# Strassen parts inside w1 at another byte distance from their stationary operand, and w2's own Strassen chunks one chunk later

## The chip, the cores and the metric

One Trainium2 chip, one core. The metric is device time in microseconds of one execution of the program.

## What is computed

Two transformer layers on 256 tokens of width 2048, all in float32: layer 0 mixes with stick-breaking attention, layer 1 with a sparse attention of three branches. Each layer ends with the same kind of MLP, which is where the change lies:

```python
def sqrelu_mlp(h, w1, w2):                      # w1: 2048 x 8192, w2: 8192 x 2048
    return jnp.square(jax.nn.relu(h @ w1)) @ w2

for layer in range(2):
    h = h + mixer(rms_norm(h, norm_g), ...)
    h = h + sqrelu_mlp(rms_norm(h, mlp_norm_g[layer]), mlp_w1[layer], mlp_w2[layer])
```

## The kernel before

Weights stream from HBM in chunks of 512 KB: a chunk is a tile `raw` of 128 partitions x 1024 floats (two blocks of 128 rows by 512 columns). ScalarE writes a rounded copy `hi`, VectorE the rest `lo = raw - hi` (`split`), and TensorE takes the product from three matmuls in fp32r: hi by the activations' high part, hi by their low part, lo by their high part. The pools hold five `raw`, four `hi` and four `lo` tiles.

Each MLP runs four feed-forward groups `fg` of 2048 columns. `group1(fg)` multiplies by w1: four blocks of eight chunks in `chunk_T`, each 24 matmuls at L186 with the weights as the **stationary** operand (128x128) and the activations `xs` as the **moving** one (256 columns). `group2(fg)` multiplies by w2 in `chunk_N`, 12 matmuls at L156 with the activations `yhi`, `ylo` stationary and 512 columns of the weights moving. Two of w2's four column blocks of each group are computed with a Strassen scheme instead: `chunk_S`, 21 matmuls at L253 with activations stationary (`yhi`, `ylo`, or prepared sums `ss`) and 256 columns of weights or of weight sums moving. Below, a *w1 chunk* is one call of `chunk_T`, an *N chunk* one of `chunk_N`, an *S chunk* one of `chunk_S`.

S chunks are never run in a row. Block 3 of group `fg - 1` is run inside `group1(fg)`, for fg of 1 to 3: `proj_T` calls `step` after the third and the sixth chunk of each block, so eight S chunks lie between 32 w1 chunks. Block 2 is run inside `group2(fg)`, between N chunks, at positions that the line with `j >= ...` sets (L464). An S chunk costs VectorE five operations (L226, L232, L233, L234 `slo`, and L136 on `ts`), ScalarE two (L231 `shi`, L134 on `ts`); `shi` and `slo` have one buffer each.

Every `hi`, `lo`, `shi` and `slo` tile has 64 spare elements (`PAD`), and its data begin at an offset into the tile:

```python
PAD = 64
NEAR, FAR, TURN, SUM, SUM0 = 0, 16, 8, 48, 60       # elements of 4 bytes
```

These tiles are a whole number of 256 bytes long in each partition, and so are all rows and columns that a matmul steps over, so the offset sets where stationary and moving operand lie towards each other, modulo 256 bytes. In the built program, as stationary start minus moving start modulo 256 bytes (the *distance* below): N chunks 0 (NEAR), w1 chunks 64 (FAR), the first w1 chunk of a `group1` with fg > 0 32 (TURN), S chunks inside w1 64 (SUM), S chunks inside w2 16 for the six matmuls on `shi` (SUM0) and 64 for the other fifteen (SUM). While one matmul runs, the next one's weights are loaded; where a w1 chunk is followed by an S chunk the last moving operand and the next stationary one are 0 apart, and from an S chunk back to w1 128.

The Tile framework's scheduler sets the order of instructions on each engine; each engine runs its own in order, and semaphores join them.

Of the kernel before, what the change touches and what calls it, by code (L numbers as in the profile page):

```python
# [39 lines left out]
def hybrid_kernel(  # L40
# [65 lines left out]
    def pump():  # L106
        if beside:
            b = beside[0]
            b[2] += b[1] / KC
            while b[2] >= 1:  # L110
                b[2] -= 1
                y = next(b[0], b)
                if y is b:
                    beside.remove(b)
                if y:
                    break
# [11 lines left out]
    NEAR, FAR, TURN, SUM, SUM0 = 0, 16, 8, 48, 60  # L128

    def split(raw, o=(NEAR, NEAR)):  # L130
        n = KC * NB
        view = lambda t, a: t[:, a:a + n].rearrange("p (k n) -> p k n", k=raw.shape[1])
        hi = view(whi.tile([P, n + PAD], F32R, tag="hi", name="hi"), o[0])
        nc.scalar.activation(hi, raw, AF.Copy)  # L134
        lo = view(wlo.tile([P, n + PAD], F32R, tag="lo", name="lo"), o[1])
        nc.vector.tensor_tensor(lo, raw, hi.bitcast(F32), op=OP.subtract)  # L136
        return hi, lo

    def load(src, k0, nk, n0, nn):
        raw = wraw.tile([P, nk, nn], F32, tag="raw", name="raw")  # L140
        nc.sync.dma_start(
            raw, src[k0 * P:(k0 + nk) * P, n0:n0 + nn].rearrange("(k p) n -> p k n", p=P)
        )
        return raw
# [4 lines left out]
    def bank(pool, tag):  # L149
        return pool.tile([P, NB], F32, tag=tag, name=tag)  # L150
# [54 lines left out]
    def proj_Th(src, n0):  # L205

        ps = bank(acc, "acc")
        proj_T([ps], src, n0, 2 * KC)
        return ps
# [4 lines left out]
            dst, ps.rearrange("p (m t) -> p m t", m=2), row.unsqueeze(1).to_broadcast([P, 2, T]), op=OP.mult  # L214
        )

    def chunk_S(ps, src, k0, n0, first, last, ahi, alo, shi, slo, koff=0, o=SUM0):


        W = NB // 2  # L220
        raw = load(src, k0, KC, n0, NB)
        flat = raw.rearrange("p k n -> p (k n)")

        ts = wsum.tile([P, 4, W], F32, tag="ts", name="ts")
        b12 = flat[:, 3 * W:].unsqueeze(1).to_broadcast([P, 2, W])
        nc.vector.tensor_tensor(ts[:, :2, :], flat[:, W:3 * W].rearrange("p (a n) -> p a n", a=2), b12, op=OP.subtract)  # L226
        hi, lo = [
            wsum.tile([P, 3 * W + PAD], F32R, tag=n, name=n, bufs=1)[:, a:a + 3 * W]
            for n, a in (("shi", o), ("slo", SUM))
        ]  # L230
        nc.scalar.activation(hi, flat[:, :3 * W], AF.Copy)  # L231
        nc.vector.tensor_tensor(ts[:, 2, :], ts[:, 0, :], flat[:, 2 * W:3 * W], op=OP.add)  # L232
        nc.vector.tensor_tensor(ts[:, 3, :], flat[:, :W], ts[:, 2, :], op=OP.subtract)  # L233
        nc.vector.tensor_tensor(lo, flat[:, :3 * W], hi.bitcast(F32), op=OP.subtract)  # L234
        thi, tlo = split(ts, (SUM, SUM))
        k = k0 - koff
        y = lambda a, kk, t: a[:, k + kk, t * P:(t + 1) * P]
        s = lambda a, i: a[:, k // KC, i, :]
        b = lambda w, i: w[:, i * W:(i + 1) * W]
        trivial = [  # L240
            (0, y(ahi, 1, 0), y(alo, 1, 0), b(hi, 2), b(lo, 2)),
            (1, y(ahi, 0, 0), y(alo, 0, 0), b(hi, 0), b(lo, 0)),
            (2, s(shi, 3), s(slo, 3), b(hi, 1), b(lo, 1)),
        ]
        sums = [
            (6, s(shi, 2), s(slo, 2), thi[:, 0, :], tlo[:, 0, :]),
            (4, s(shi, 0), s(slo, 0), thi[:, 1, :], tlo[:, 1, :]),
            (5, s(shi, 1), s(slo, 1), thi[:, 2, :], tlo[:, 2, :]),
            (3, y(ahi, 0, 1), y(alo, 0, 1), thi[:, 3, :], tlo[:, 3, :]),
        ]  # L250

        def mm(i, a, w, s, e):
            nc.tensor.matmul(ps[i], a, w, start=s, stop=e, skip_group_check=True)  # L253

        for i, xh, xl, wh, wl in trivial + sums:

            mm(i, xh, wh, first and i in (0, 1, 6, 4), False)
            mm(i, xl, wh, False, False)
        pump()
        for i, xh, xl, wh, wl in trivial + sums:  # L260
            mm(i, xh, wl, False, last)
        pump()

    def banks_S(pool, tag):

        W = NB // 2
        bs = [bank(pool, tag) for _ in range(4)]
        half = lambda j, i: bs[j][:, i * W:(i + 1) * W]
        return bs, [half(0, 0), half(1, 0), half(1, 1), half(2, 0), half(2, 1), half(3, 1), half(3, 0)]
# [127 lines left out]
    def mlp(l, layer, junk, done, last=None):  # L397
# [9 lines left out]
        def in_S(fg, nb, o):  # L407

            for i in range(NK):
                if i == 0:  # L410
                    bs, s = banks_S(att, "att")
                chunk_S(s, w2, fg * KD + i * KC, nb * NB, i == 0, i == NK - 1, yhi, ylo, ss[:, 0], ss[:, 1],
                        koff=fg * KD, o=o)
                if i == NK - 1:
                    add_S(nb, bs, s, junk)
                yield
# [29 lines left out]
        def group2(fg, end):  # L446

            blocks = (0, 1, 3) if end else (0, 1)
            side, si = in_S(fg, 2, SUM0), 0
            for j in range(len(blocks) * NK):  # L450
                nb, i = blocks[j // NK], j % NK
                if i == 0:
                    ps = [bank(acc, "acc") for _ in range(NT)]
                out = last is not None and end and nb == 3
                chunk_N(ps, w2, fg * KD + i * KC, nb * NB, i == 0, i == NK - (2 if out else 1), yhi, ylo,
                        koff=fg * KD, by_token=out and i == NK - 1)
                if i == NK - 1:
                    if out:
                        add_out(nb, ps, last)
                        return  # L460
                    add_h(nb, ps)
                    if end and nb == 3:
                        done(nb, (att, "att"))
                if si < NK and j >= (3 + 1.75 * si if end else 2 + 1.6 * si):  # L464
                    next(side)
                    si += 1
                    if si == NK and end:
                        for n in range(3):
                            done(n, (att, "att"))

        spawn(rows(), 1)
        NK = KD // KC
        for fg in range(DFF // D):
            group1(fg, in_S(fg - 1, 3, SUM) if fg else None)
            group2(fg, fg == DFF // D - 1)


    with tc.tile_pool(name="sbp", bufs=2) as sp:
# [12 lines left out]
        with tc.manual_schedule(engines={mybir.EngineType.PE, mybir.EngineType.DVE, mybir.EngineType.Activation,  # L491
# [47 lines left out]
            for i in range(NX):  # L539
# [4 lines left out]
                first, last = i == 0, i + 1 == NX  # L544
# [142 lines left out]
    with tc.tile_pool(name="nsa", bufs=2) as ap, ExitStack() as last:  # L687
        w_in = nsa_w_in[0]
        C0 = D
        first = ExitStack()  # L690
# [252 lines left out]
        for i in range(2):  # L943
            cT = cp.tile([P, G, T], F32, tag="cT", name="cT", bufs=1)
            for b in range(2):
                ps = proj_Th(w_in, C0 + i * NB + b * T)
# [61 lines left out]
        for g in range(G):  # L1008
            ps = [bank(acc, "acc") for _ in range(NT)]
# [16 lines left out]
            ps = proj_N(w_in, g * NB)  # L1026
# [46 lines left out]
```

## Time and profile before

| | |
|---|---|
| three runs | 2176.88, 2178.96, 2179.82 us (median 2178.96) |
| profiled execution | 2184.23 us, its span from first to last instruction 2180.6 us |
| TensorE (PE) busy | 2168.8 us, 99% of the span, 14914 matmuls |
| VectorE (DVE) busy | 1593.0 us, 73% |
| ScalarE (ACT) busy | 1188.2 us, 54% |
| HBM read | 401.83 MB, 185 GB/s over the span |

A busy matmul row overlaps the next one (it holds its latency), so busy time doesn't tell whether TensorE runs at its best rate. That is read from starts: the time from the start of one row to the start of another, divided by the matmuls between them, is called *spacing* below.

### The profile page before, as it was taken

The numbers are of one execution on the slowest core, as the hardware profiler recorded it, in microseconds if no ns is written. First come the engines' busy times: TensorE is split into PE (matmuls) and PEld (weight loads), VectorE is DVE, ScalarE is ACT, GpSimd is POOL, SyncE is SP. The second block draws the span as 40 slices with busy tenths as digits, with TensorE's granted clock in tenths as the row PEclk, the third lists the DMA queues.
The fourth block names the chain that finished last, engine by engine and source line by source line (L and its number), as shares of the span: only waits on it lengthen the run. The fifth ranks groups of instructions, "written<-read, shape, count | busy, mean of one in ns | idle before, by whom it ended". The sixth has DMA issues, their size and how long they took to land.

```text
span 2180.6 us, 37293 instructions
## 1 busy us (share of the span) xinstructions
PE 2168.8 (99%) x14914; PEld 2000.9 (92%) x14914; DVE 1593.0 (73%) x2190; ACT 1188.2 (54%) x1591; POOL 42.5 (2%) x75
## 2 busy tenths in 40 slices
PE   9999999999999999999999999999999999999999
PEld 9999988998998999999898888889989989999998
DVE  4655556668778878778777877755778788787786
ACT  5555565545555455555546666654554545554553
POOL 0000000000000000000000011000000000000000
PEclk9999999999999999999999999999999999999999
DMA  7655555665665665665667554456556556656664
GB/s 223 204 176 173 164 174 176 187 198 178 209 194 183 203 194 185 221 194 182 201 183 221 164 145 135 137 164 188 181 201 190 191 182 215 198 176 212 194 196 162
DMA packets 260790, 406.35 MB, mean 186 GB/s; under 512 B 13188, under 2 KB 91912, under 8 KB 260616
## 3 DMA queue, kind: packets, MB, share of 16 engines
q1 hardware_dynamic: 259800, 403.52, 59.3%
q8 instruction: 116, 1.90, 0.4%
q10 hardware_dynamic: 816, 0.46, 0.1%
q14 instruction: 58, 0.48, 0.1%
HBM read 401.83 MB, written 2.10 MB: 185 GB/s over the span
## 4 chain that ended last, share of the span: by engine, by line
PE 96%; DVE 2%; DMA 1%; ACT 0%; issue 0%; POOL 0%; DVEq 0%; ACTq 0%; SPq 0%; POOLq 0%
PE acc L186 43%; PE acc L156 35%; PE att L253 12%; PE att L156 1%; DMA raw<-in_mlp_w_dram 1%; DVE lo L136 1%; PE att L310 1%; PE att L905 1%; PE att L897 0%; PE att L898 0%; PE att L899 0%; PE att L592 0%; PE att L640 0%; PE att L851 0%; DVE slo L234 0%
## 5 line engine op out<-in xcount | busy, mean ns | idle before, releaser
L134 ACT ACTIVATE hi<-raw 128x1024 fp32r<-128x1024 f32 x639 | 672.8, 1057 | 503.4 <-PE acc L186 229.0
L136 DVE TENSOR_TENSOR lo<-raw,hi 128x1024 fp32r<-128x1024 f32 x639 | 776.4, 1221 | 224.5 <-ACT hi L134 206.2
L186 PE MATMUL acc<-xs,hi 128*128 128x256 f32 x5360 | 679.5, 280 | 1.9 <-ACT hi L134 1.9
L186 PEld LDWEIGHTS acc<-xs,hi 128*128 128x128 f32 x5360 | 647.8, 189 | 3.1 <-ACT hi L134 2.1
L186 PE MATMUL acc<-xs,lo 128*128 128x256 f32 x2680 | 366.5, 280 | 0.0
L186 PEld LDWEIGHTS acc<-xs,lo 128*128 128x128 f32 x2680 | 335.7, 189 | 0.0
L156 PE MATMUL acc<-hi,yhi 128*128 128x512 f32 x828 | 324.9, 393 | 0.0
L156 PE MATMUL acc<-hi,ylo 128*128 128x512 f32 x828 | 323.3, 391 | 0.0
L134 ACT ACTIVATE hi<-ts 128x1024 fp32r<-128x1024 f32 x112 | 118.4, 1057 | 195.0 <-DVE ts L233 121.8
L156 PE MATMUL acc<-lo,yhi 128*128 128x512 f32 x828 | 223.1, 391 | 0.0
L226 DVE TENSOR_TENSOR ts<-raw 128x512 f32<-128x512 f32 x112 | 77.4, 691 | 169.9 <-DMA raw<-in_mlp_w_dram 169.7
L156 PEld LDWEIGHTS acc<-lo,yhi 128*128 128x128 f32 x828 | 154.6, 188 | 31.9 <-issue 0.4
L156 PEld LDWEIGHTS acc<-hi,ylo 128*128 128x128 f32 x828 | 155.7, 188 | 29.5 <-DVE ylo L297 0.2
L156 PEld LDWEIGHTS acc<-hi,yhi 128*128 128x128 f32 x828 | 155.6, 188 | 29.6 <-ACT yhi L296 0.2
L156 PE MATMUL acc<-hi,xs 128*128 128x512 f32 x704 | 177.2, 392 | 0.0
L156 PEld LDWEIGHTS acc<-hi,xs 128*128 128x128 f32 x704 | 130.4, 188 | 26.5
L136 DVE TENSOR_TENSOR lo<-ts,hi 128x1024 fp32r<-128x1024 f32 x112 | 136.6, 1220 | 12.0 <-ACT hi L134 11.2
L231 ACT ACTIVATE shi<-raw 128x768 fp32r<-128x768 f32 x112 | 94.0, 839 | 65.0 <-DMA raw<-in_mlp_w_dram 38.3
L234 DVE TENSOR_TENSOR slo<-raw,shi 128x768 fp32r<-128x768 f32 x112 | 106.6, 952 | 0.0
L156 PE MATMUL acc<-lo,xs 128*128 128x512 f32 x352 | 97.5, 397 | 0.0
L253 PE MATMUL att<-hi,ss 128*128 128x256 f32 x672 | 94.8, 277 | 0.0
L253 PEld LDWEIGHTS att<-hi,ss 128*128 128x128 f32 x672 | 85.5, 188 | 0.0
(248 smaller groups left out, 2132.2 us busy)
## 6 DMA issues: line engine op xcount, KB each, us to landing
raw<-in_mlp_w_dram SPq DMA_DIRECT2D x512, 512.0 KB, 4.3
raw<-in_sb_w_qkv_dram SPq DMA_DIRECT2D x95, 512.0 KB, 3.8
raw<-in_nsa_w_in_dram SPq DMA_DIRECT2D x50, 512.0 KB, 3.8
raw<-in_sb_w_out_dram SPq DMA_DIRECT2D x32, 512.0 KB, 4.0
raw<-in_nsa_w_in_dram SPq DMA_DIRECT2D x64, 256.0 KB, 3.4
raw<-in_nsa_w_out_dram SPq DMA_DIRECT2D x32, 512.0 KB, 3.7
w1t<-in_nsa_cmp_w_dram SPq DMA_DIRECT2D x8, 512.0 KB, 4.8
h<-in_x_dram SPq DMA_DIRECT2D x8, 256.0 KB, 4.8
```

What stands on the lines that cost most here:

```text
L134: nc.scalar.activation(hi, raw, AF.Copy)
L136: nc.vector.tensor_tensor(lo, raw, hi.bitcast(F32), op=OP.subtract)
L156: mm = lambda a, b, k, t, s, e: nc.tensor.matmul(ps[t], a[:, k, t * P:(t + 1) * P], b, start=s, stop=e)
L186: nc.tensor.matmul(o, w[:, kk, m * P:(m + 1) * P], x[:, k0 + kk, :], start=s, stop=e, skip_group_check=True)
L226: nc.vector.tensor_tensor(ts[:, :2, :], flat[:, W:3 * W].rearrange("p (a n) -> p a n", a=2), b12, op=OP.subtract)
L231: nc.scalar.activation(hi, flat[:, :3 * W], AF.Copy)
L234: nc.vector.tensor_tensor(lo, flat[:, :3 * W], hi.bitcast(F32), op=OP.subtract)
L253: nc.tensor.matmul(ps[i], a, w, start=s, stop=e, skip_group_check=True)
L310: nc.tensor.transpose(ps[:, j * T + t * P:j * T + (t + 1) * P], h[:, t, (kp + j) * P:(kp + j + 1) * P], ident)
L905: nc.tensor.transpose(ptp[:w, j * P:(j + 1) * P], src(j), ident)
```

## The change

`chunk_S` takes a pair of offsets, for `shi` and for the other three tiles, instead of one for `shi` alone. Inside w1 all four now begin at FAR (64 bytes) instead of SUM (192 bytes); since `yhi`, `ylo` and `ss` don't move, the distance becomes 192 instead of 64, and in the built program the step from an S chunk back to w1 is 0 instead of 128; from w1 to an S chunk it stays 0. Inside w2 the offsets stay (SUM0, SUM), and for the groups fg 0 to 2 the S chunks are placed after N chunks 3, 5, 6, 8, 9, 11, 12, 14 (counted from 0) instead of 2, 4, 6, 7, 9, 10, 12, 14. The last group keeps its rule.

```diff
-    def chunk_S(ps, src, k0, n0, first, last, ahi, alo, shi, slo, koff=0, o=SUM0):
+    def chunk_S(ps, src, k0, n0, first, last, ahi, alo, shi, slo, koff=0, o=(SUM0, SUM)):
...
-            for n, a in (("shi", o), ("slo", SUM))
+            for n, a in (("shi", o[0]), ("slo", o[1]))
...
-        thi, tlo = split(ts, (SUM, SUM))
+        thi, tlo = split(ts, (o[1], o[1]))
...
-            side, si = in_S(fg, 2, SUM0), 0
+            side, si = in_S(fg, 2, (SUM0, SUM)), 0
...
-                if si < NK and j >= (3 + 1.75 * si if end else 2 + 1.6 * si):
+                if si < NK and j >= (3 + 1.75 * si if end else 3 + 1.5 * si):
...
-            group1(fg, in_S(fg - 1, 3, SUM) if fg else None)
+            group1(fg, in_S(fg - 1, 3, (FAR, FAR)) if fg else None)
```

The order of instructions changes only in `group2` of fg 0 to 2 and at its edges. TensorE at the start of w2 in the first MLP, before (row 706 ends the third N chunk, 707 begins the first S chunk):

```order
704 L156 MATMUL acc<-hi,yhi 128x512
705 L156 MATMUL acc<-hi,ylo 128x512
706 L156 MATMUL acc<-lo,yhi 128x512 x4
707 L253 MATMUL att<-shi,yhi 128x256
708 L253 MATMUL att<-shi,ylo 128x256
```

and of the change:

```order
712 L156 MATMUL acc<-hi,ylo 128x512
713 L156 MATMUL acc<-hi,yhi 128x512
714 L156 MATMUL acc<-hi,ylo 128x512
715 L156 MATMUL acc<-lo,yhi 128x512 x4
716 L253 MATMUL att<-shi,yhi 128x256
```

One N chunk more stands ahead of the first S chunk. After it the N chunks between S chunks were 2, 2, 1, 2, 1, 2, 2 and are 2, 1, 2, 1, 2, 1, 2: a single N chunk between two S chunks comes three times instead of twice.

VectorE in the same group, before, from the evacuation of the first N block (L366) over the fifth S chunk's `slo` (250) to the sixth's (259):

```order
248 L366 TENSOR_TENSOR h<-acc,h 128x512 x2
249 L136 TENSOR_TENSOR lo<-ts,hi 128x1024
250 L234 TENSOR_TENSOR slo<-raw,shi 128x768
251 L136 TENSOR_TENSOR lo<-raw,hi 128x1024
252 L232 TENSOR_TENSOR ts<-ts,raw 128x256
253 L233 TENSOR_TENSOR ts<-raw,ts 128x256
254 L136 TENSOR_TENSOR lo<-ts,hi 128x1024
255 L226 TENSOR_TENSOR ts<-raw 128x512
256 L136 TENSOR_TENSOR lo<-raw,hi 128x1024
257 L232 TENSOR_TENSOR ts<-ts,raw 128x256
258 L233 TENSOR_TENSOR ts<-raw,ts 128x256
259 L234 TENSOR_TENSOR slo<-raw,shi 128x768
```

and of the change, from the fourth S chunk's `slo` (245) to the fifth's (253), which now make the pair around that evacuation:

```order
245 L234 TENSOR_TENSOR slo<-raw,shi 128x768
246 L136 TENSOR_TENSOR lo<-raw,hi 128x1024
247 L366 TENSOR_TENSOR h<-acc,h 128x512 x2
248 L136 TENSOR_TENSOR lo<-ts,hi 128x1024
249 L226 TENSOR_TENSOR ts<-raw 128x512
250 L136 TENSOR_TENSOR lo<-raw,hi 128x1024
251 L232 TENSOR_TENSOR ts<-ts,raw 128x256
252 L233 TENSOR_TENSOR ts<-raw,ts 128x256
253 L234 TENSOR_TENSOR slo<-raw,shi 128x768
```

The evacuation has moved in between the two `slo` of a pair with one N chunk between them, and one L232 and one L233 less stand there.

## Rows read from the trace of the kernel before

**Rows 1.** The page: the span, TensorE's busy time, the chain of work that ended last by engine and by line, and the first w1 row of the costliest groups (its columns: busy us, mean ns of one).

```profile
span 2180.6 us, 37293 instructions
PE 2168.8 (99%) x14914; PEld 2000.9 (92%) x14914; DVE 1593.0 (73%) x2190; ACT 1188.2 (54%) x1591; POOL 42.5 (2%) x75
...
PE 96%; DVE 2%; DMA 1%; ACT 0%; issue 0%; POOL 0%; DVEq 0%; ACTq 0%; SPq 0%; POOLq 0%
PE acc L186 43%; PE acc L156 35%; PE att L253 12%; PE att L156 1%; DMA raw<-in_mlp_w_dram 1%; DVE lo L136 1%; PE att L310 1%; PE att L905 1%; PE att L897 0%; PE att L898 0%; PE att L899 0%; PE att L592 0%; PE att L640 0%; PE att L851 0%; DVE slo L234 0%
...
L186 PE MATMUL acc<-xs,hi 128*128 128x256 f32 x5360 | 679.5, 280 | 1.9 <-ACT hi L134 1.9
```

**Rows 2.** The w1 matmuls of line L186 in two stretches, 425 to 478 us (first group of the first MLP, no S chunk in it) and 572 to 582 us (second group, between S chunks): durations of one in ns, least, median and most; then busy time by stretch, where the column after PEld is the granted clock.

```profile
L186 PE MATMUL acc<-xs,hi x312: 275/276/277, 424.8 to 477.2; 128*128 128x256 f32 x156
...
L186 PE MATMUL acc<-xs,hi x62: 278/281/282, 571.9 to 581.9; 128*128 128x256 f32 x62
...
425.00:470.00 45.00, 45.00 (x400) 45.00 (x399) 1.00 0.70 197
572.20:585.90 13.70, 13.70 (x118) 13.70 (x118) 1.00 0.57 163
```

**Rows 3.** The timeline of TensorE in the first group's w1 (start us, us, instruction, count). The two rows begin neighbouring chunks of 24 matmuls.

```profile
442.89 1.98 PE L186 MATMUL acc<-xs,hi 128*128 128x256 f32 x16
...
445.61 1.98 PE L186 MATMUL acc<-xs,hi 128*128 128x256 f32 x16
```

**Rows 4.** The same view at the start of the second group's w1: the chunk at distance 32, the chunk after it, the first matmul of the first S chunk (three w1 chunks in), and the first w1 matmul after it.

```profile
550.27 2.06 PE L186 MATMUL acc<-xs,hi 128*128 128x256 f32 x16
...
553.11 1.98 PE L186 MATMUL acc<-xs,hi 128*128 128x256 f32 x16
...
558.55 0.28 PE L253 MATMUL att<-shi,yhi 128*128 128x256 f32 x1
...
561.02 1.22 PE L186 MATMUL acc<-xs,hi 128*128 128x256 f32 x9
```

**Rows 5.** The same view later in that group: the start of the second S chunk, of the five w1 chunks after it, of the third S chunk, of the w1 chunks after that, and of the first two N chunks (12 matmuls each) behind the whole group.

```profile
569.51 0.29 PE L253 MATMUL att<-shi,yhi 128*128 128x256 f32 x1
...
571.91 0.63 PE L186 MATMUL acc<-xs,hi 128*128 128x256 f32 x4
...
586.04 0.29 PE L253 MATMUL att<-shi,yhi 128*128 128x256 f32 x1
...
588.44 2.04 PE L186 MATMUL acc<-xs,hi 128*128 128x256 f32 x16
...
659.80 0.40 PE L156 MATMUL acc<-hi,yhi 128*128 128x512 f32 x1
...
662.55 0.39 PE L156 MATMUL acc<-hi,yhi 128*128 128x512 f32 x1
```

**Rows 6.** The same view where chunks of the w1 kind (L186, distance 64) follow N chunks directly, at the first projection of layer 1. The rows begin neighbouring chunks of 24.

```profile
1093.00 2.05 PE L186 MATMUL acc<-xs,hi 128*128 128x256 f32 x16
...
1095.83 2.05 PE L186 MATMUL acc<-xs,hi 128*128 128x256 f32 x16
```

**Rows 7.** The same view at other distances with 256 moving columns: an S chunk in w2 (six matmuls at distance 16 from 494.59, fifteen at 64 from 495.30, then an N chunk); 32 matmuls of L759, whose distance goes down by 32 bytes at each, through all eight multiples of 32 four times; and eight matmuls of L164 at distance 0.

```profile
494.59 0.28 PE L253 MATMUL att<-shi,yhi 128*128 128x256 f32 x1
...
495.30 0.85 PE L253 MATMUL att<-hi,ss 128*128 128x256 f32 x6
...
497.00 0.39 PE L156 MATMUL acc<-hi,yhi 128*128 128x512 f32 x1
...
1191.10 0.28 PE L759 MATMUL att<-ws,bs 128*120 128x256 f32 x1
...
1194.88 0.40 PE L156 MATMUL acc<-hi,xs 128*128 128x512 f32 x1
...
2175.36 0.40 PE L164 MATMUL acc<-hi,ylo 128*128 128x256 f32 x2
...
2176.32 0.40 PE L164 MATMUL acc<-lo,yhi 128*128 128x256 f32 x2
```

**Rows 8.** Who waited for whom in 551 to 661 us (us in total, times, longest), and busy time of the engines in that stretch (TensorE, weight loads, VectorE, ScalarE, GpSimd, granted clock, share of DMA, GB/s).

```profile
ACT hi L134 <- PE acc L186: 30.8, 20, 1.8
...
551.00:661.00 110.00, 110.00 (x938) 109.78 (x937) 89.13 (x113) 57.15 (x58) 0.00 (x0) 1.00 0.64 199
```

**Rows 9.** TensorE's waits for `slo` from 484 us to the end (us in total, times, longest), as its weight loads have them, and one in the timeline, in the sixth S chunk of the first `group2`.

```profile
PEld att L253 <- DVE slo L234: 3.7, 5, 1.3
...
530.87 0.50 PE L253 MATMUL att<-slo,yhi 128*128 128x256 f32 x2 [0.60 <-DVE slo L234]
```

**Rows 10.** The timeline of VectorE in the first `group2`: what one S chunk, one N chunk's `lo` and the evacuation of a block (two operations) take.

```profile
504.69 0.69 DVE L226 TENSOR_TENSOR ts<-raw 128x512 f32<-128x512 f32 x1 [1.41 <-DMA raw<-in_mlp_w_dram]
505.41 0.43 DVE L232 TENSOR_TENSOR ts<-ts,raw 128x256 f32<-128x256 f32 x1
505.87 0.42 DVE L233 TENSOR_TENSOR ts<-raw,ts 128x256 f32<-128x256 f32 x1
506.22 1.22 DVE L136 TENSOR_TENSOR lo<-ts,hi 128x1024 fp32r<-128x1024 f32 x1
507.35 0.95 DVE L234 TENSOR_TENSOR slo<-raw,shi 128x768 fp32r<-128x768 f32 x1
...
519.79 1.28 DVE L366 TENSOR_TENSOR h<-acc,h 128x512 f32<-128x512 f32 x2
```

## Prediction

> **What bounds the kernel now.** I read the page's busy times and chain first. TensorE is busy 99% of the span and holds 96% of the chain that ended last; the w1 matmuls of L186 alone are 43% of it [rows 1]. So the kernel is as long as its matmuls take, and an edit pays only if it changes how fast they follow each other or takes away one of TensorE's few waits. A busy share of 99% doesn't say that the rate is the best one, so I next compared one line with itself in two stretches. The w1 matmuls last 276 ns in the first group, where no S chunk is mixed in, and 281 ns in the second; the granted clock is 1.00 in both, so it is not the clock [rows 2]. The timeline turns that into spacing:
>
> - first group: 24 matmuls in 445.61 - 442.89 = 2.72 us, **113.3 ns** each [rows 3]. I call this rate quiet.
> - second group after an S chunk: 120 matmuls in 586.04 - 571.91 = 14.13 us, **117.75 ns** each [rows 5]. I call this rate slow. Nothing in these rows is marked as a wait.
>
> VectorE and ScalarE are not behind it. In 551 to 661 us VectorE is busy 89.13 of 110 us, ScalarE 57.15, and ScalarE waits 30.8 us for TensorE to give buffers back [rows 8]: the producers run ahead.
>
> Next, where the slow rate begins. The second group's w1 starts with one chunk at distance 32, (553.11 - 550.27) / 24 = 118.3 ns. The two chunks after it, at 64, take (558.55 - 553.11) / 48 = 113.3 ns: quiet. Then comes the first S chunk, also at 64: (561.02 - 558.55) / 21 = 117.6 ns, slow [rows 4]. From there to the end of the group every w1 chunk is slow, while the second and third S chunk take (571.91 - 569.51) / 21 = 114.3 and (588.44 - 586.04) / 21 = 114.3 ns, nearly quiet [rows 5]. So distance 64 has two rates, and which one holds depends on how the stretch was entered:
>
> - a step over 0 out of quiet w1 gave a slow S chunk [rows 4]; out of slow w1 it gave a nearly quiet one [rows 5]. N chunks, whose distance is 0 throughout, are followed by a slow w1-like chunk, (1095.83 - 1093.00) / 24 = 117.9 ns [rows 6].
> - a step over 128 (S chunk back to w1) gave slow w1 both times, out of a slow S chunk [rows 4, 5] and out of nearly quiet ones [rows 5].
>
> **The change part by part.** No matmul, byte or DMA is added or removed, so all terms are rates and waits.
>
> *w1 after S chunks.* Of a group's 32 x 24 = 768 w1 matmuls the first 72 come ahead of any S chunk and keep their rates. The other 696 now come behind a step over 0 instead of 128. As a check of the price now: 561.02 to 659.80 is 98.78 us, holds these 696 and seven S chunks of 2.40 us, which leaves 81.98 us or 117.8 ns each [rows 4, 5]. Quiet they would take 696 x (117.75 - 113.33) ns = 3.07 us less. Six groups (fg 1 to 3, two MLPs) make **18.4 us**. Bounds: 0 if they stay slow, and 18.4 us, since 113.3 is the fastest 256-column spacing in these rows. VectorE's cover survives: 89.1 of 107 us is 83%.
>
> Which of the two? By the rows, a step over 0 swaps the rate: slow before, quiet after. So it hangs on how the S chunk at 192 runs. No stretch of before stays at 192. With 256 columns, distance 16 takes (495.30 - 494.59) / 6 = 118.3 ns, distance 0 takes (2176.32 - 2175.36) / 8 = 120.0, and the 32 matmuls that walk through all eight multiples of 32, 192 among them, take (1194.88 - 1191.10) / 32 = 118.1 [rows 7]; 32 takes 118.3 [rows 4]. Only 64 has shown 113.3. So I expect the S chunks at 192 to be slow, and w1 after them quiet. That 64 is reached quiet out of an unsettled rate is also what the end of an S chunk in w2 shows: fifteen matmuls in 497.00 - 495.30 = 1.70 us, 113.3 ns, behind six at distance 16 [rows 7], and what w1 shows behind its chunk at 32 [rows 4].
>
> Against this stands a rule of the Trainium skill, "TensorE: Matmul & The Clock Gate", Step-by-step: what each phase is for: TensorE has one SBUF read port for the moving operand and another for weights, and "Loading the next tile's weights doesn't steal SBUF read bandwidth from the running matmul." By that rule where the two operands lie would not matter. The trace disagrees as far as it shows one shape at 113.3 and 117.75 ns at the same clock [rows 3, 5]; what in the memory makes the difference, no row shows.
>
> *The S chunks in w1.* 8 x 21 = 168 matmuls a group. Now the first chunk costs 21 x 4.3 ns and seven cost 21 x 1.0 ns above quiet, 0.24 us a group. At 192 the bounds are quiet (0) and the 120.0 ns of distance 0 (168 x 6.7 = 1.12 us). I take the walk's 118.1 ns, the only row with 192 in it: 168 x 4.8 = 0.80 us. Six groups: 6 x (0.80 - 0.24) = **+3.4 us**, between -1.4 and +5.3.
>
> *The S chunks of w2, one N chunk later.* The price now is TensorE's wait for `slo`: 3.7 us in five waits, at most 1.3 each [rows 9]. It falls in the sixth S chunk, a single N chunk behind the fifth. Between the two `slo` VectorE has two lo of raw, one lo of ts, L226, two pairs of L232 and L233 and the `slo` itself: 3 x 1.22 + 0.69 + 2 x 0.85 + 0.95 = 7.0 us [rows 10], while TensorE runs one S chunk and one N chunk, 497.00 - 494.59 = 2.41 us [rows 7] and 662.55 - 659.80 = 2.75 us [rows 5], 5.2 us in all. In the changed order the pair around the evacuation has 3 x 1.22 + 0.69 + 0.85 + 1.28 + 0.95 = 7.4 us of VectorE work: no better. There are three such pairs instead of two, but the first S chunk comes 2.7 us later behind w1's own evacuations, which gives VectorE a lead. The signs oppose each other; I take **0**. Bounds: all waits gone, -3.7 us; a wait of the longest kind, 1.3 us, in each of six groups, 7.8 - 3.7 = +4.1 us. Queued behind a late `slo` on VectorE are the next N chunk's lo and the next sums; TensorE waits for those a chunk later at the earliest.
>
> Sum: -18.4 + 3.4 + 0 = **-15.0 us**. In the profiled execution that is 2184.23 to 2169.2 us and the span 2180.6 to 2165.6; the profiled execution lies 5.3 us over the median of the timed runs, so I take the difference off the median: 2178.96 - 15.0 = **2164 us**. With the bounds of its two smaller terms this case reaches from 2160 (-18.4 + 3.0 - 3.7; 3.0 is the S chunks at 117.75) to 2170 (-18.4 + 5.3 + 4.1).
>
> **The rivals.**
>
> *Both quiet.* 192 may settle like 64, and w1 too: -18.4 - 1.4 = -19.8, 2159 us. For it: 64 shows that a distance can be quiet. Against it: by the swap, a quiet S chunk would leave w1 slow.
>
> *Quiet parts, slow w1.* By the same swap, if 192 is quiet, w1 stays at 117.75: -1.4 us, 2177.5. With it goes the case that the distance does nothing to rates at all, by which all stays: 2179 us, give or take the waits of w2. For the first, the step over 0 behind N chunks gives slow [rows 6]; against the second, rows 3 and 5. The Trainium skill's rule above would be this second case; I give it 5 in 100.
>
> *Part of w1.* The first S chunk of a group is entered from quiet w1 and the others not, so the groups may get quiet in part: half of the 18.4 us, 2173 us.
>
> *Slower.* At 192 the S chunks lock at the 120.0 ns of distance 0, and the step over 0 out of such a rate leaves w1 at 117.75: +5.3 us, 2184 us. It decides, passing 0.2% (4.4 us), once the S chunks in w1 take over about 119 ns while w1 keeps its rate. For it: two unlike steps into w1 out of S chunks both gave slow before.
>
> **How the numbers follow.** Main case 53 in 100, both quiet 8, part of w1 5, w1 slow or nothing changed 24, slower 10. Under 0.2% a measurement of this kernel can't tell a change from none (its three runs span 0.13%). Faster: 53 + 8 + 5 = 66. Slower: the 10, and 2 of the unchanged case when the waits of w2 all lengthen: 12. The same: 22. The range 2157 to 2181 holds the first three cases and the unchanged one except its upper end; what it leaves out is the slower case and some 7 in 100 at the ends. The main case's own range is 2160 to 2170.
>
> **What would show it.** Right: in groups 2 to 4 of each MLP w1 chunks behind an S chunk take 2.72 us and L186 lasts 276 ns there, L186's mean falls from 280 ns to about 277; S chunks in w1 take 2.47 to 2.52 us instead of 2.40; TensorE's waits for `slo` stay within some 8 us. Wrong: L186 still at 281 ns between S chunks (the step over 0 doesn't free it), S chunks in w1 at 2.38 us (192 is quiet), or waits of TensorE in w1 for hi or lo (the cover is gone, and the faster rate is taken back).

## The result and the profile after

The changed kernel takes **2167.24 us** (median of five executions, 2164.97 to 2171.18) against 2178.96 us: a ratio of 0.995, 95% interval [0.9935, 0.9964], 11.7 us. Run once more beside other kernels it gave 2167.36 us, 0.9935 [0.9921, 0.9948]. The prediction was 2164 us, so size and sign came out; none of its three terms took the value that it forecast, as the trace shows. Of the changed kernel's page: the span, TensorE's busy time, its chain, and the first w1 group ([rows 1] before):

```profile
span 2163.3 us, 37297 instructions
PE 2153.7 (100%) x14914; PEld 1986.6 (92%) x14914; DVE 1594.5 (74%) x2190; ACT 1201.7 (56%) x1591; POOL 42.6 (2%) x75
...
PE 99%; DVE 0%; POOL 0%; ACT 0%; issue 0%; DVEq 0%; ACTq 0%; POOLq 0%
...
L186 PE MATMUL acc<-xs,hi 128*128 128x256 f32 x5360 | 671.4, 278 | 1.9 <-ACT hi L134 1.9
```

TensorE is still busy for all of the span. L186's mean fell from 280 to 278 ns, not to 277, and in the chain VectorE's 2% and the DMA's 1% have gone to 0. The timeline of TensorE in the second group's w1 shows why it is 278 (first row: the chunk at distance 32; L253 `shi,yhi`: the start of an S chunk; the L186 row behind it: the first w1 matmul after it; last row: the first N chunk; [rows 4, 5] show the same place before):

```profile
546.30 2.06 PE L186 MATMUL acc<-xs,hi 128*128 128x256 f32 x16
...
554.58 0.28 PE L253 MATMUL att<-shi,yhi 128*128 128x256 f32 x1
...
556.97 2.05 PE L186 MATMUL acc<-xs,hi 128*128 128x256 f32 x16
...
565.45 0.28 PE L253 MATMUL att<-shi,yhi 128*128 128x256 f32 x1
...
567.92 1.99 PE L186 MATMUL acc<-xs,hi 128*128 128x256 f32 x16
...
581.54 0.28 PE L253 MATMUL att<-shi,yhi 128*128 128x256 f32 x1
...
583.92 2.05 PE L186 MATMUL acc<-xs,hi 128*128 128x256 f32 x16
...
654.24 0.40 PE L156 MATMUL acc<-hi,yhi 128*128 128x512 f32 x1
```

The first S chunk comes out of quiet w1 and takes (556.97 - 554.58) / 21 = 113.8 ns a matmul; the 72 w1 matmuls behind it take (565.45 - 556.97) / 72 = 117.8 ns: slow. The second S chunk, out of slow w1, takes 2.47 / 21 = 117.6 ns, and the 120 behind it 13.62 / 120 = 113.5 ns: quiet. Then it begins again (2.38 us, and slow w1). The granted clock is 1.00 in this stretch. All eight S chunks of all six groups do this: **at distance 192 an S chunk keeps the rate of the w1 matmuls ahead of it, and the step back to w1 swaps it.** So three of every eight w1 chunks are slow (12 of a group's 29 behind the first S chunk), not none. The group lasts 654.24 - 546.30 = 107.94 us; before it was 659.80 - 550.27 = 109.53 [rows 4, 5]. Six times 1.59 us is 9.5 us.

Of TensorE's waits from 484 us to the end this is all that the view of the waits still lists for the engine:

```profile
PE att L770 <- DVE hs L766: 0.9, 1, 0.9
PE att L805 <- DVE kc L801: 0.5, 1, 0.5
```

The waits for `slo` [rows 9] are gone. In the sixth S chunk of the first `group2`, where TensorE waited before, VectorE's `slo` ends at 526.1 us and is first used at 529.75 us:

```profile
525.18 0.95 DVE L234 TENSOR_TENSOR slo<-raw,shi 128x768 fp32r<-128x768 f32 x1
...
529.75 0.39 PE L253 MATMUL att<-slo,yhi 128*128 128x256 f32 x2
```

The two profiled executions differ by 17.3 us of span, more than the medians. The one before lost 3.1 us in its first 24 us, where both kernels run the same instructions. Busy time by stretch, before and then after (the column behind the five engines is the granted clock):

```profile
15.00:22.00 7.00, 5.13 (x31) 5.05 (x31) 3.33 (x4) 3.52 (x8) 0.00 (x0) 0.76 0.63 191
```

```profile
15.00:22.00 7.00, 6.52 (x57) 6.52 (x58) 4.93 (x7) 5.20 (x14) 0.00 (x0) 1.00 0.85 277
```

For every kernel below I added up the same things over its whole trace: for the matmuls of L186 and of L253, the spacing above 113.33 ns ("rate"), and apart from it the gaps over 60 ns ahead of an S chunk's matmul ("waits at S chunks"). All in us; a rate is lost time, so less is better. The ratio is that of the timed executions.

| kernel | ratio to before [95%] | median | rate of w1 kind | rate of S | waits at S chunks |
|---|---|---|---|---|---|
| before | | 2178.96 | 21.3 | 3.8 | 4.4 |
| changed | 0.995 [0.9935, 0.9964] | 2167.24 | 10.8 | 4.4 | 0 |
| changed again | 0.9935 [0.9921, 0.9948] | 2167.36 | 10.9 | 4.4 | 0 |
| distance alone | 1.0003 [0.9987, 1.002] | 2180.89 | 10.9 | 4.6 | 17.0 |
| places alone | 0.9994 [0.9981, 1.0008] | 2179.52 | 21.2 | 3.6 | 0 |
| no chunk at 32 | 0.9969 [0.9957, 0.9981] | 2173.84 | 15.3 | 4.5 | 1.5 |
| distance alone, six raw | 1.0002 [0.9988, 1.0017] | 2181.59 | 10.9 | 4.6 | 8.0 |
| last four at 16 | 0.9943 [0.9922, 0.9964] | 2168.29 | 3.9 | 2.9 | 14.9 |
| last four at 16, six raw | 1.0011 [0.9999, 1.0023] | 2182.62 | 4.5 | 3.3 | 18.8 |
| last four at 16, even places | 0.9922 [0.9906, 0.9938] | 2163.84 | 4.0 | 3.1 | 7.7 |
| even places | 0.9933 [0.992, 0.9946] | 2167.95 | 11.1 | 4.6 | 5.4 |
| last four at 16, even in the last group | 0.9921 [0.9907, 0.9936] | 2164.34 | 3.9 | 2.9 | 3.1 |

Two executions of the places alone, at 2823 and 3075 us with a granted clock of 0.71 and 0.65, are left out of its row. The profiled execution is one of several, and waits differ between executions (the kernel with the distance alone ran in 2173.8 to 2189.8 us). The rates agree within 0.3 us in all traces of the same offsets but one (the last four at 16 with six raw buffers, where two stretches of w1 stayed slow). From before to changed the rows of the table give 10.5 us less for w1, 0.6 more for S chunks and 4.4 less of waits; with the 3.1 us of the start that is 17.4 of the 17.3. The medians are closer than the profiled executions, 2184.23 and 2164.97 us: of their 11.7 us the rates are 9.9, since the rates don't change from trace to trace, which leaves 1.8 us, by this estimate, for waits and all else.

### The profile page after: what moved, and what is told of

Same layout as the page of the kernel before. It is cut to its first block, busy times and chain, and to the rows that moved or that the text cites. A ratio compares the mean times of both kernels' runs of the same rounds, so it can differ in the third digit from the quotient of the medians.

```text
span 2163.3 us, 37297 instructions
## 1 busy us (share of the span) xinstructions
PE 2153.7 (100%) x14914; PEld 1986.6 (92%) x14914; DVE 1594.5 (74%) x2190; ACT 1201.7 (56%) x1591; POOL 42.6 (2%) x75
## 4 chain that ended last, share of the span: by engine, by line
PE 99%; DVE 0%; POOL 0%; ACT 0%; issue 0%; DVEq 0%; ACTq 0%; POOLq 0%
PE acc L186 43%; PE acc L156 37%; PE att L253 13%; PE att L156 1%; PE att L905 1%; PE att L310 1%; PE att L897 0%; PE att L898 0%; PE att L899 0%; PE att L592 0%; PE att L640 0%; PE att L851 0%; PE att L853 0%; PE att L852 0%; PE att L829 0%; PE att L759 0%
## 5 line engine op out<-in xcount | busy, mean ns | idle before, releaser
L186 PE MATMUL acc<-xs,hi 128*128 128x256 f32 x5360 | 671.4, 278 | 1.9 <-ACT hi L134 1.9
L186 PEld LDWEIGHTS acc<-xs,hi 128*128 128x128 f32 x5360 | 640.5, 188 | 3.2 <-ACT hi L134 2.1
L186 PE MATMUL acc<-xs,lo 128*128 128x256 f32 x2680 | 362.2, 278 | 0.0
L186 PEld LDWEIGHTS acc<-xs,lo 128*128 128x128 f32 x2680 | 331.7, 188 | 0.0
L134 ACT ACTIVATE hi<-ts 128x1024 fp32r<-128x1024 f32 x112 | 118.6, 1059 | 142.7 <-DVE ts L233 65.5
L226 DVE TENSOR_TENSOR ts<-raw 128x512 f32<-128x512 f32 x112 | 77.0, 690 | 106.0 <-DMA raw<-in_mlp_w_dram 105.7
L253 PE MATMUL att<-hi,ss 128*128 128x256 f32 x672 | 95.2, 277 | 0.0
L253 PEld LDWEIGHTS att<-hi,ss 128*128 128x128 f32 x672 | 85.8, 188 | 0.0
```

Source lines behind the costliest of these rows:

```text
L186: nc.tensor.matmul(o, w[:, kk, m * P:(m + 1) * P], x[:, k0 + kk, :], start=s, stop=e, skip_group_check=True)
```

## Experiments

**Each part alone.** First the distance, with w2's S chunks at their old places:

```diff
-                if si < NK and j >= (3 + 1.75 * si if end else 3 + 1.5 * si):
+                if si < NK and j >= (3 + 1.75 * si if end else 2 + 1.6 * si):
```

> The distance alone: S chunks inside w1 at 192, w2's S chunks at their old places. In the trace of the changed kernel the rate swapped at every S chunk in w1: quiet w1, quiet S chunk, three slow w1 chunks, slow S chunk, five quiet w1 chunks. Theory (the distance carries the gain, by rates): the same pattern here, 17 of the 29 w1 chunks behind the first S chunk of a group quiet, 6 x 408 x 4.42 ns = 10.8 us less, minus 0.7 us for S chunks at 117.9 ns, so about 2169 us, 10 us under the kernel before; TensorE's waits for slo stay at 2 to 5 us. Rival (the new places carry it): within 3 us of the kernel before.

Measured: 2180.89 us, ratio 1.0003, no gain at all. The rates are those of the changed kernel to 0.2 us, as the theory said; the time is the rival's, but not for its reason. The gain is eaten in w2 (the view of the waits from 484 us to the end, here and below: VectorE's for raw chunks, and TensorE's for `slo`; us in total, times, longest):

```profile
DVE ts L226 <- DMA raw<-in_mlp_w_dram: 189.1, 81, 4.8
...
PEld att L253 <- DVE slo L234: 14.4, 10, 3.3
```

The longest, in TensorE's timeline, and the busy time by stretch around it:

```profile
2134.22 0.50 PE L253 MATMUL att<-slo,yhi 128*128 128x256 f32 x2 [3.06 <-DVE slo L234]
...
2135.78 0.63 PE L156 MATMUL acc<-hi,yhi 128*128 128x512 f32 x1
...
2136.20 0.63 PE L156 MATMUL acc<-hi,ylo 128*128 128x512 f32 x1
```

```profile
2131.00:2134.20 3.20, 0.17 (x2) 0.00 (x0) 3.13 (x6) 1.06 (x1) 0.00 (x0) 1.00 0.01 4
2135.30:2139.40 4.10, 4.10 (x13) 3.22 (x12) 1.50 (x3) 1.57 (x2) 0.00 (x0) 0.58 0.94 331
```

The wait costs twice: 3.06 us, and then eight matmuls of N chunks at 2136.20 - 2135.78 = 0.42 us instead of 0.23, at a granted clock of 0.58 (most of it at the lower of the two levels, 1.2 GHz), some 1.6 us more. VectorE's `slo` is late there because it is itself queued behind L226, which waited for its raw chunk. The load of that chunk was issued only when the `slo` before it was done and gave a raw buffer back, at 2125.6 us (SyncE's waits name that `slo`); L226 got the chunk 4.9 us later:

```profile
2124.63 0.95 DVE L234 TENSOR_TENSOR slo<-raw,shi 128x768 fp32r<-128x768 f32 x1
...
2125.61 8.96 SPq L141 DMA_DIRECT2D raw<-in_mlp_w_dram  x4
...
2130.55 0.69 DVE L226 TENSOR_TENSOR ts<-raw 128x512 f32<-128x512 f32 x1 [2.70 <-DMA raw<-in_mlp_w_dram]
...
2133.22 0.95 DVE L234 TENSOR_TENSOR slo<-raw,shi 128x768 fp32r<-128x768 f32 x1
```

In sum the trace has 10.4 us less of rates of w1 and 12.6 us more of waits at S chunks than before. Of its 17.0 us of such waits 13.7 lie in groups 0 to 2, whose places differ from the changed kernel's. The longest, above, lies in the last group of the second MLP (3.3 us in all there), whose places and order of instructions are the same in the changed kernel, where it doesn't occur in either trace; so that one isn't due to the group's own places alone. The profiled execution took 2185.25 us against the median of 2180.89, so its waits are more than those of a usual one.

Then the places alone:

```diff
-            group1(fg, in_S(fg - 1, 3, (FAR, FAR)) if fg else None)
+            group1(fg, in_S(fg - 1, 3, (SUM, SUM)) if fg else None)
```

> The places alone: S chunks inside w1 at 64 as before, w2's S chunks one N chunk later. Theory: w1 at 117.75 ns behind every S chunk as before; TensorE's waits for slo (3.7 us as the weight loads have them) gone, so 1.5 to 4 us under the kernel before, 2175 to 2177.5 us. Rival (the places carry the gain): 8 to 12 us under it. Rival (the waits of slo are only in the profiled execution): within 1 us of before.

Measured: 2179.52 us, ratio 0.9994 with an interval from 4.1 us faster to 1.7 us slower. The same kernel was run again for its trace.

> The places alone, a second look, for the trace (the first profile fell into a throttled execution). Expected: w1 at 117.75 ns behind every S chunk as before, TensorE's waits for slo under 1.5 us (before: 3.7), VectorE's waits for raw at L226 below the 168.6 us of before; a span of 2173 to 2178 us. If the waits stay at 3 to 4 us, the places do nothing by themselves.

Measured: 2176.05 us, span 2174.3 us; TensorE waits for no `slo` at all, and VectorE waits much less for raw chunks:

```profile
DVE ts L226 <- DMA raw<-in_mlp_w_dram: 112.0, 76, 3.7
```

So the places do take the waits away in this execution, as the theory said; how much that is worth by itself in timed executions, between 0 and 4 us, the interval doesn't settle. What the two runs do settle: **the parts don't add up.** Alone they give +0.03% and -0.06%, together -0.5% and -0.65%. The distance makes w1 faster, as its rates show in every trace, but with the old places it gains no time, neither here nor with six raw buffers below; with the new places it does.

**Does the rate swap, or is it the place in the block?** In the changed kernel the slow chunks are always the same three of a block, so something beside them there could be at fault. Without the chunk at 32, w1 starts slow, and a swap would turn every rate around:

```diff
-                proj_T(ps, w1, fg * D + fb * NB, turn=fg > 0 and fb == 0,
+                proj_T(ps, w1, fg * D + fb * NB, turn=False,
```

> The changed kernel without the chunk at distance 32 at the start of a group's w1 (all w1 chunks at 64), so that w1 starts behind N chunks at the slow rate. Parity theory (a step over 0 between w1 and S chunk swaps the rate, both ways): all rates are inverted: three slow w1 chunks, slow S chunk, three quiet, quiet S chunk, five slow, and so on: 20 slow w1 chunks in a group instead of 12, and no chunk at 118.2: 6 x (8 x 24 x 4.42 - 24 x 4.9) ns = +4.4 us over the changed kernel, about 2171.6 us. Rival (place theory: the three chunks between the two S chunks of a block are slow because of what runs beside them there, the evacuation of the block before among it): the same three chunks stay slow, the time falls by up to 0.7 us, and nothing is inverted.

Measured: 2173.84 us, 0.9969 (forecast: about 2171.6). TensorE's timeline in the second group's w1 (same rows as for the changed kernel):

```profile
546.22 2.05 PE L186 MATMUL acc<-xs,hi 128*128 128x256 f32 x16
...
554.70 0.28 PE L253 MATMUL att<-shi,yhi 128*128 128x256 f32 x1
...
557.17 1.99 PE L186 MATMUL acc<-xs,hi 128*128 128x256 f32 x16
...
565.34 0.28 PE L253 MATMUL att<-shi,yhi 128*128 128x256 f32 x1
...
567.73 2.05 PE L186 MATMUL acc<-xs,hi 128*128 128x256 f32 x16
...
581.86 0.28 PE L253 MATMUL att<-shi,yhi 128*128 128x256 f32 x1
```

The first 72 w1 matmuls take 8.48 / 72 = 117.8 ns, the next 72 (565.34 - 557.17) / 72 = 113.5, the 120 after them (581.86 - 567.73) / 120 = 117.8. Every rate is inverted, in all six groups, and w1 loses 15.3 instead of 10.8 us: 4.5 us, where 4.4 were forecast. The place theory falls: the same work lies beside the same chunks. What was wrong in the words of the expectation is "both ways": the step into an S chunk is 0 as well and does not swap at 192; the step out does.

**Other distances.** `chunk_S` got a third offset, for the low part of the sums (the last four matmuls), and each of the six groups its own three:

```diff
-        thi, tlo = split(ts, (o[1], o[1]))
+        thi, tlo = split(ts, (o[1], o[2]))
...
+    WHERE = (
+        (None, (0, 0, 0), (32, 32, 32), (56, 56, 56)),
+        (None, (FAR, FAR, 60), (FAR, FAR, 8), (FAR, FAR, 48)),
+    )
```

> The changed kernel with another distance for the S chunks in each of the six groups that have them in w1: in the first MLP all parts at 0, at 128 and at 32; in the second MLP 192 with the last four matmuls (on the low part of the sums) at 16, at 224 and at 64. Parity theory: only a step over 0 back to w1 swaps, and the chunk at distance 32 unsettles the rate and leaves 64 quiet behind it. At 0 and 128 no step back to w1 is 0, so w1 behind S chunks keeps one rate for the whole group, as before; S chunks at 0 take 120.0 ns. At 32 (118.2 ns) and with the last four at 16 or 224 the rate is unsettled when w1 begins, and w1 behind every S chunk is quiet, 113.3 ns in all 29 chunks, 3.07 us less than before in a group. With the last four at 64 the step back is 128 and w1 is slow everywhere, as before. Place theory: in all six groups only the three chunks between the S chunks of a block are slow.

Spacing of an S chunk and state of the w1 chunks behind it, for the whole group each (one execution, 2180.71 us; its groups differ, so the time tells nothing):

| S chunks in w1 at | step back to w1 | S, ns | w1 behind |
|---|---|---|---|
| 0 | 64 | 119.9 | slow after all |
| 128 | 192 | 118.6 | slow after all |
| 32 | 96 | 118.4 | **quiet after all** |
| 192, last four at 16 | 80 | 113.4, then 117 | **quiet after all** |
| 192, last four at 224 | 32 | 113.4 once, then 118.0 | slow after all |
| 192, last four at 64 | 128 | as at 192, then 118 | swaps, as at 192 |

TensorE's timeline in the group with the last four at 16 (starts of S chunks and of the w1 behind them):

```profile
1638.91 0.28 PE L253 MATMUL att<-shi,yhi 128*128 128x256 f32 x1
...
1641.30 1.99 PE L186 MATMUL acc<-xs,hi 128*128 128x256 f32 x16
...
1649.48 0.28 PE L253 MATMUL att<-shi,yhi 128*128 128x256 f32 x1
...
1651.88 1.99 PE L186 MATMUL acc<-xs,hi 128*128 128x256 f32 x16
...
1665.49 0.28 PE L253 MATMUL att<-shi,yhi 128*128 128x256 f32 x1
```

8.18 us for 72 and 13.61 us for 120 w1 matmuls are 113.6 and 113.4 ns: quiet behind the first S chunk of a block and the second. Four expectations held, two fell: 224 does not leave w1 quiet as 16 and 32 do, and a step of 128 does not always leave it slow. The step alone is no rule, then; what is left is an empirical map. It moved only the S chunks' moving operand, and so can't tell the distance from that operand's own offset. For the distance speaks that w1 chunks (weights 64 bytes into their tile, stationary) and the S chunks of before (weights 192 bytes in, moving), both at distance 64, show the same two rates, to about 1 ns.

**All of w1 quiet.** The changed kernel with the last four at 16 (offsets `(FAR, FAR, SUM0)` inside w1):

> The changed kernel with the last four matmuls of every S chunk inside w1 (on the low part of the sums) at distance 16, the other 17 at 192. Rates, from the group that had this in the map: w1 quiet (113.3 ns) behind every S chunk, S chunks 17 at 113.4 and four at 117 ns. Against the changed kernel that is 6 x 288 x 4.42 ns = 7.6 us for w1 and 6 x 0.27 = 1.6 us for S chunks, 9.2 us less: 2158 us, if the producers keep pace. Rival (the producers are close to their limit, so that a faster w1 turns into waits for slo and loads in w2): the rates come as said, waits for slo of 5 to 12 us appear, and the time is 2162 to 2172 us.

Measured: 2168.29 us, 0.9943. The rates came as said (3.9 and 2.9 us in the table, 8.4 us less than changed), and no time was won, since the rival held: 10.8 us of waits for `slo` in the profiled execution (2175.85 us, 7.6 over the median).

```profile
DVE ts L226 <- DMA raw<-in_mlp_w_dram: 189.9, 88, 5.1
...
PEld att L253 <- DVE slo L234: 10.8, 8, 5.0
```

```profile
2123.62 0.80 PE L253 MATMUL att<-slo,yhi 128*128 128x256 f32 x2 [4.80 <-DVE slo L234]
...
2125.70 0.63 PE L156 MATMUL acc<-hi,ylo 128*128 128x512 f32 x1
```

This is the distance alone over again, one step further on: 4.80 us of wait in the last group, and matmuls at half the rate behind it.

**Is it the number of raw buffers?** In the MLPs every sixth chunk gets a tile of its own, for the distance alone and for the last four at 16:

```diff
-        raw = wraw.tile([P, nk, nn], F32, tag="raw", name="raw")
+        six = wsum is not None and next(loads) % 6 == 5
+        raw = wsum.tile([P, nk, nn], F32, tag="raw6", name="raw", bufs=1) if six else wraw.tile([P, nk, nn], F32, tag="raw", name="raw")
```

> The distance alone, once more, with a sixth buffer for the raw chunks of the MLPs (every sixth chunk goes to a tile of its own). With five, w1 ran at the changed kernel's rates, but TensorE's waits for slo grew to 14.4 us as the weight loads have them, and VectorE waited 189 us for raw at L226 (168.6 before). Theory (the loads run too late because five raw buffers are all that may be in flight or held): the waits for slo fall to under 4 us, and the time to 2166 to 2171 us, 10 us under the five-buffer one. Rival (VectorE's own work between the slo of a pair of S chunks with one N chunk between them is what is late): the waits stay at 8 to 14 us and the time at 2176 to 2182 us.

> The same with the sixth raw buffer. If five raw buffers are what makes the loads late: waits for slo under 3 us and 2155 to 2160 us. If VectorE's own work between two slo is what is late: no better than with five buffers.

Measured: 2181.59 and 2182.62 us, the second 14 us more than with five buffers. The waits for `slo` were 6.4 us in the first, less than the 14.4 with five buffers, and 12.9 us in the second, more than the 10.8. The first comparison is of single executions, of 2176.66 and 2185.25 us; the medians of the two kernels differ by 0.7 us, and the ratios not at all. VectorE waited longer for raw chunks, not shorter:

```profile
DVE ts L226 <- DMA raw<-in_mlp_w_dram: 206.2, 79, 5.1
```

```profile
DVE ts L226 <- DMA raw<-in_mlp_w_dram: 209.1, 78, 5.8
```

The theory of the five buffers gets no support from the times. It isn't refuted cleanly: with the sixth tile the scheduler also ordered VectorE's and ScalarE's instructions anew, so the two effects are mixed.

**Is it the single N chunk between two S chunks?** Even places, one S chunk after every second N chunk, for the last four at 16 and for the changed kernel:

```diff
-                if si < NK and j >= (3 + 1.75 * si if end else 3 + 1.5 * si):
+                if si < NK and j >= (2 + 2 * si if end else 1 + 2 * si):
```

> The kernel with the last four matmuls of an S chunk in w1 at distance 16 (w1 quiet everywhere, but waits for slo of 10.8 us in its trace), with w2's S chunks evenly spaced: one after every second N chunk (N chunks 1, 3, ... 15; in the last group 2, 4, ... 16), so that no single N chunk lies between two S chunks. Theory (VectorE's work between the slo of two S chunks with one N chunk between them is what is late, 7.0 to 7.4 us of work against 5.2 us of TensorE): the waits for slo fall to under 2 us and the time to 2155 to 2161 us. Rival (the loads are late whatever the places; the sixth buffer already did not help, so another limit of the loads): waits for slo stay above 6 us, the time stays at 2164 to 2172 us.

> The changed kernel with the same even places. Its trace shows no wait for slo, with the slo of each S chunk in w2 ready 1 to 6 us ahead. Theory: the lead of the least early slo grows to 2 us or more, and the time stays within 3 us of the changed kernel, 2164 to 2169 us. Rival (loads late whatever the places): waits come back, 2170 us or more.

> The changed kernel itself once more, beside the other two on one chip, for its ratio to the kernel before: 0.993 to 0.9965, 2164 to 2172 us, no wait of TensorE for slo in the trace. If waits for slo turn up in this execution, their absence in the first trace was luck.

Measured: 2163.84, 2167.95 and 2167.36 us. With the last four at 16 the waits for `slo` fall from 10.8 to 1.8 us, as the theory said, but 3.0 us of waits for `hi` of the sums appear, the longest in the second S chunk of the first MLP's second group (1.68 us); in all 7.7 us of waits at S chunks are left of 14.9. The time lies at the edge between the two forecasts, and settles neither:

```profile
PEld att L253 <- DVE slo L234: 1.8, 6, 0.4
```

```profile
671.05 0.95 PE L253 MATMUL att<-hi,ss 128*128 128x256 f32 x6 [1.68 <-ACT hi L134]
```

In the changed kernel the even places win nothing: the time is as forecast, but 2.1 us of waits for `slo` and 2.2 us for `hi` of the sums appear, against the lead that I forecast. The changed kernel itself has none in its second trace either, so one lucky execution doesn't explain their absence.

**Even places in the last group alone**, again with the last four at 16 (`2 + 2 * si if end else 3 + 1.5 * si`):

> The last four matmuls of an S chunk in w1 at distance 16, w2's places of the changed kernel in groups 0 to 2, and the even places in the last group alone (an S chunk after N chunks 2, 4, ... 16). In the trace with the changed places everywhere, the last group lost about 9 us of the gain: one wait for slo of 5 us, some 2 us of small ones, and 2 us of N chunks at half the clock behind it; with even places everywhere it lost under 2 us, but groups 0 to 2 had waits of 1.9 and 1.5 us on the second S chunk. Theory (each group's waits come from its own places): the last group's waits fall to under 3 us, the others' stay at 4 to 7 us, 2159 to 2165 us. Rival (a wait taken away in one place turns up in another): 2165 to 2170 us.

Measured: 2164.34 us, 0.9921, inside the theory's range and within 1 us of the rival's. TensorE's timeline has no wait left in the last group; the three over 0.2 us that are left at S chunks lie in the third group of the second MLP:

```profile
1911.79 0.62 PE L253 MATMUL att<-lo,ss 128*128 128x256 f32 x3 [0.80 <-DVE lo L136]
...
1925.63 0.50 PE L253 MATMUL att<-slo,yhi 128*128 128x256 f32 x2 [0.74 <-DVE slo L234]
...
1939.57 0.50 PE L253 MATMUL att<-slo,yhi 128*128 128x256 f32 x2 [0.65 <-DVE slo L234]
```

That fits the theory that a group's waits come from its own places, but doesn't show it: groups 0 to 2 have the same places as in the run with the last four at 16 above, and their waits at S chunks are 3.1 us here and 6.5 there, so single executions differ by several us. This and the even places everywhere are the fastest kernels here, some 3 us under the changed one by the medians; their intervals overlap with its own, so that step is not clear of noise.

## Why the prediction came out, point by point

- **What bounds the kernel: right.** TensorE's rate, not its busy share: busy went from 99% to 100% while 10 us left w1.
- **"I expect the S chunks at 192 to be slow, and w1 after them quiet": the step that failed.** I had one row with 192 in it, the walk over all distances at 118.1 ns, and took its mean for a property of 192. The trace shows that 192, like 64, has both rates. The swap that I read off [rows 4, 5] would not have mended it: there the step into an S chunk, over 0, swaps the rate, and so would make the S chunk slow and w1 quiet, as forecast. At 192 that step keeps the rate, and only the step out swaps it; no row of before could show that. The outcome is quiet S chunk, slow w1, slow S chunk, quiet w1, so 12 of 29 chunks slow. It comes nearest to the rival "part of w1", at 5 in 100; and the argument against "both quiet", that a quiet S chunk leaves w1 slow, held for every second S chunk. Term: -18.4 forecast, -10.5 measured.
- **S chunks in w1: mis-sized.** +3.4 us forecast, +0.6 measured, for the same reason: half of them run at 113.4 ns.
- **w2, one N chunk later: the value failed, the bound nearly held.** I set a longer first lead against three pairs instead of two and took 0. No wait is left in two traces of the changed kernel and one of the places alone, -4.4 us against a bound of -3.7 (the matmul gaps count a little more than the rows of waits). That the lead did it is argued, not shown; the even places, which shorten it and leave no such pair, have waits again.
- **"VectorE's cover survives": right for w1, wrong for what follows.** Within w1 TensorE waits for nothing. But I priced the places at the old speed of w1. With the old places a faster w1 costs 12.6 us of waits at S chunks in its trace, three times my bound of +4.1, and in the timed executions the whole gain. The two edits are one change with two halves, and a sum of separate terms could not show it.
- **The sum.** -15.0 came near -11.7 because an overestimate in w1 (7.9 us) met two errors the other way (2.8 for S chunks, and 4.4 for waits in the profiled executions or 1.8 by the medians). The sign and the place rest on evidence; the closeness is luck.
- **The rule of the Trainium skill** ("TensorE: Matmul & The Clock Gate", Step-by-step: what each phase is for), by which a weight load takes no bandwidth from the running matmul: the runs speak against the consequence, drawn from it in the prediction, that the place of the operands is free. The same S chunk takes 113.4 to 119.9 ns by its offset alone, at a granted clock of 1.00.

Open: what in the memory makes the two rates, and what sets how late the raw chunks come. A faster w1 isn't all of it: with the new places VectorE waits about as long for them in the changed kernel as at the slower w1 of the places alone. VectorE's wait for them from 484 us on is 104.1 and 115.1 us in the two traces of the changed kernel, 112.0 with the places alone, 168.6 before, 132.4 without the chunk at 32, and 149 to 209 us in all others; the sixth buffer did not shorten it.

## What to carry to other kernels

Compare one line's spacing between stretches of the same clock before believing that a busy engine is at its best; "Perfetto Trace Analysis" of the Trainium skill (Identifying the Most-Contended Engine) warns of matmul busy time as a measure, and here it stood at 99 to 100% through all of it. When a rate has two values, follow the states through a whole period of the pattern, not one transition. And when an edit makes the bound engine faster, reprice every wait downstream at the new speed: test each half of a change alone, since a half that looks worthless may be what lets the other pay.

## What the hardware showed that I had not expected

- A stretch of fp32r matmuls with 256 columns at distance 64 or 192 has two stable rates, 113.3 and 117.8 ns, and keeps one for more than a hundred matmuls on end; an S chunk at 192 keeps it on the way in and swaps it on the way out, 48 times of 48 in each of six traces. At 0, 16, 32, 128 and 224 the low one was not seen: runs of 4 to 21 matmuls, each counted to the start of the matmul behind it, have means of 116.5 to 120 ns.
- A pause can change the rate too. In the trace of the even places one stretch of w1 runs 48 matmuls at 117.8 ns; then one starts 197 ns after the one before it (at 1895.71 us), and the rest of the stretch runs at 113.3. A pause of about the same length in a quiet stretch (the last four at 16) left it quiet.
- Four matmuls at distance 16 are enough to leave w1 quiet behind them, 48 times of 48 in three traces and 46 in a fourth (six raw buffers); four at 224 leave it slow, 8 times of 8.
- A wait of some 3 us can be followed by a granted clock at the lower level. After 3.06 us without matmuls it was 0.58 over the next 4.1 us, and N-chunk matmuls went from 0.23 to 0.42 us. The Trainium skill's page "TensorE: Matmul & The Clock Gate" (Part 1: The HAM clock gate) has these two levels and the fall after idle time, and the trace agrees; a wait of 1.59 us in the same trace was not followed by it. The length of the wait alone doesn't decide: in the traces with six raw buffers a wait of 2.10 us was followed by the lower level and one of 2.76 us wasn't.
